# RMS norms that scale by a diagonal matrix inside the transposing products, with split passes held behind the norm's steps

## The chip, the cores and the metric

The kernel runs on one core of a Trainium2 chip. The metric is the device time of one execution in microseconds (us), smaller is better. The kernel before takes 2280.77 us, the median of 3 runs (2278.39 to 2280.96).

## The reference, cut to what matters

Two blocks of two layers each run on 256 tokens of width 1024, all in float32. Every large product is preceded by an RMS norm of the residual x; these norms are what the change rewrites.

```python
def rms_norm(x, w):
    y = x * lax.rsqrt(jnp.mean(x * x, axis=-1, keepdims=True) + EPS)
    return y * w
# first block, layers i = 0, 1
h = rms_norm(x, norm_mix_w[i])
mem_n = rms_norm(mem, mem_norm_w[i])
proj = h @ w_in[i]                       # gated delta rule (i=0), sparse attention (i=1)
x = x + concat([mix(proj), memory_attention(proj, mem_n)]) @ w_out[i]
x = x + conv_glu(rms_norm(x, norm_ffn_w[i]), w_up, conv_w, conv_b, w_down)
# second block, layers l = 0, 1; shift, scale and gate come from cond @ w_ada + b_ada
x = rms_norm(x, final_norm_w)            # between the blocks
h = rms_norm_2(x, norm1_g[l]) * (1 + scale1) + shift1
x = x + gate1 * (merged(h @ w_in[l]) @ w_out[l])
h2 = rms_norm_2(x, norm2_g[l]) * (1 + scale2) + shift2
x = x + gate2 * hierarchical_moe(h2)     # 32 experts
```

## The kernel before, in words

Everything is issued by one Python class in program order; a tile scheduler puts each engine's instructions in an order of its own, by dependences and its cost estimates, and each engine then runs its list strictly in that order. Weights come in units of 1 MB, tiles `raw` of 128 x 2048, loaded by SyncE (`unit`, L396) into a ring of four slots. Float32 products are made of three matmuls (`mm3`, L352 to L356): both operands are split into a high part and a low part, and high x high, high x low and low x high are summed. The split of a weight half (1024 columns) is a copy on ScalarE (L407) and a subtraction on VectorE (L408), into tiles `whl`, of which there are four (`split`, `hilo`). A unit is thus two splits and 48 matmuls of 256 columns (`ws2`).

The activations are split once per norm, into `xh` and `xl`, eight slices k of 128 features by 256 tokens. A norm goes like this. `sums_sq` (L523) squares x on ScalarE in four pieces (two token tiles tt, two halves) with an accumulated sum. `rms` adds EPS with a GpSimd tensor_scalar (L535) and takes the power -1/2 on GpSimd (`pow_half`, L510). `to_c_in` transposes x by sixteen TensorE transposes against the identity (L555), transposes the broadcast 1/rms into a row by two more (L560), copies that row to SBUF on ScalarE (`rsrow`, L561), multiplies each slice with weight and row on VectorE (`nf`, L567), and splits the slice: `xh` on ScalarE (L407), `xl` on VectorE (L408). In the second block, where there is a shift b, xh and xl are made with the bias (L571, L572). Then the next product's matmuls can start.

Six such norms stand between two stages of products, so that TensorE has nothing else: before the gated delta rule (`gdn`, the start of the program), before conv_glu of layer 0 and of layer 1, before the sparse attention, and before layers 0 and 1 of the second block (`layer2`). The first of those two is joined with the norm between the blocks (`mid_norm`, L594 to L596, and its `finish`, L602, which rescales x). This text calls them the six pauses. Two more norms (of mem) and the last one stand beside other work.

In both conv_glu's the modulation of the second block is computed on the side: `ada` loads 24 units `adaw` per layer on the same SyncE queue and adds each up on VectorE (L1172, the first of a group L1174), a few per chunk c of the eleven chunks (list NADA). At the program's start `start` and `masks` load x, the constants and four masks before the first weight unit is asked for (L638 to L641, L349, L396).

Of the kernel before, what the change touches and what calls it, by code (L numbers as in the profile page):

```python
# [38 lines left out]
GAP = 6  # L39
NADA = (2, 3, 2, 3, 2, 3, 2, 3, 3, 3, 3)  # L40
# [260 lines left out]
class Net:  # L301
    def __init__(self, ctx, tc, I, out, dbg=None):
# [11 lines left out]
        self.dtag = "acc"  # L314

# [83 lines left out]
    def split(self, src, n=1024):  # L399
        t = self.spl.tile([128, 2, 1024], F32R, name="whl")  # L400
        hi, lo = t[:, 0, :n], t[:, 1, :n]
        self.hilo(hi, lo, src)
        return hi, lo

    def hilo(self, hi, lo, src):

        self.nc.scalar.activation(hi, src, AF.Copy)  # L407
        self.nc.vector.tensor_sub(lo, src, hi.bitcast(F32))  # L408
# [103 lines left out]
    def sums_sq(self, x, tt, weight=None):  # L512
# [4 lines left out]
        for h in range(2):  # L517
            s = slice(h * 512, h * 512 + 512)
            if weight is None:
# [3 lines left out]
            nc.scalar.activation(junk, x[:, tt, s], AF.Square, scale=1.0 / math.sqrt(D), accum_out=ms[:, h:h + 1])  # L523
# [5 lines left out]
    def rms(self, x):  # L529

        rs = self.P.tile([128, 2], F32, name="rs", bufs=2)
        for tt in range(2):
            ms = self.sums_sq(x, tt)
# [5 lines left out]
    def to_c(self, x, rs, w, b, X, tag="mm"):  # L539

        self.nm += 1
        with self.tc.tile_pool(name=f"nrm{self.nm}", bufs=1, side="right", reuse_waits="tile") as tmp:
            return self.to_c_in(tmp, x, rs, w, b, X, tag)

    def to_c_in(self, tmp, x, rs, w, b, X, tag):
        nc, (xh, xl) = self.nc, X
        row = tmp.tile([128, 256], F32, name="rsrow")
        ps = []

        def rows():  # L550
            for _ in range(KB // 2):
                ps.append(self.pst([128, 2, 256], tag=tag))
            for tt in range(2):
                for k in range(KB):
                    nc.tensor.transpose(ps[k // 2][:, k % 2, tt * 128:tt * 128 + 128], x[:, tt, k * 128:k * 128 + 128], self.ident)  # L555

        def scales():
            p = self.dense([128, 256])
            for tt in range(2):
                nc.tensor.transpose(p[:, tt * 128:tt * 128 + 128], rs[:, tt:tt + 1].to_broadcast([128, 128]), self.ident)  # L560
            nc.scalar.activation(row, p, AF.Copy)  # L561

        for part in (scales, rows) if tag == self.dtag else (rows, scales):
            part()
        for k in range(KB):
            f = tmp.tile([128, 256], F32, name="nf", bufs=2)
            nc.vector.scalar_tensor_tensor(f, ps[k // 2][:, k % 2, :], w[:, k:k + 1], row, op0=OP.mult, op1=OP.mult)  # L567
            if b is None:
                self.hilo(xh[:, k, :], xl[:, k, :], f)
            else:  # L570
                nc.scalar.activation(xh[:, k, :], f, AF.Identity, bias=b[:, k:k + 1])  # L571
                nc.vector.scalar_tensor_tensor(xl[:, k, :], f, b[:, k:k + 1], xh[:, k, :].bitcast(F32), op0=OP.add,  # L572
                                               op1=OP.subtract)
# [5 lines left out]
    def norm_x(self, x, w, X=None):  # L579

        return self.to_c(x, self.rms(x), w, None, X or self.xtiles(), self.dtag if X else "mm")

    def mid_norm(self):
# [7 lines left out]
        for tt in range(2):  # L591
            ms = self.sums_sq(self.x, tt, w2)
            r, a = rs[:, tt:tt + 1], r1[:, tt:tt + 1]
            nc.gpsimd.tensor_scalar(a, ms[:, 0:1], ms[:, 1:2], EPS, op0=OP.add, op1=OP.add)  # L594
            nc.gpsimd.tensor_scalar(r, a, EPS, ms[:, 2:3], op0=OP.mult, op1=OP.add)
            nc.gpsimd.tensor_scalar(r, r, ms[:, 3:4], None, op0=OP.add)  # L596
# [35 lines left out]
    def start(self):  # L632
# [7 lines left out]
        nc.sync.dma_start(self.consts, self.I["consts"][:, :NKEEP])  # L640
        nc.sync.dma_start(self.cols, self.I["cols"])  # L641
# [1204 lines left out]
```

## Time and profile before

| | us |
|---|---|
| median of 3 runs | 2280.77 |
| the profiled execution's own time | 2276.92 |
| its span in the trace | 2275.1 |
| busy: TensorE (PE) / VectorE (DVE) / ScalarE (ACT) / GpSimd (POOL) | 1941.0 / 1069.9 / 773.1 / 113.8 |
| mean granted TensorE clock | 0.916 of full |
| read from HBM | 649.93 MB |

The profiled execution lies 3.9 us below the median of the three runs, and about 1.8 us of its time lie outside the span. How to read the rows further down: times are counted from the start of the span; PE is TensorE's matmuls, PEld its weight loads, SPq the queue that issues DMAs. A timeline row gives the start, the length, the engine, line and operation, output <- inputs, the number of such instructions in a row, and in brackets the idle time before it and what ended that. Matmul ends are modelled, so the spacing of starts tells more than the lengths.

### The profile page before, as it was taken

How to read it: one execution, taken by the hardware profiler on the slowest of the kernel's cores; microseconds unless marked ns; L12 is line 12 of the kernel's file. 1: busy time of each engine (PE TensorE's matmuls, PEld its weight loads, DVE VectorE, ACT ScalarE, POOL GpSimd, SP SyncE). 2: the span in 40 equal slices, each digit the busy share in tenths (PEclk: the TensorE clock that was granted, in tenths of full speed). 3: DMA queues.
4: the chain of work that ended last, by engine and by line, in shares of the span. 5: the costliest groups of instructions: out<-in, count | busy, mean ns of one | idle time of the engine just before them, and what ended most of it. 6: DMA issues, size and time to landing. Idle time of an engine off the chain costs nothing. (4 is left out here: it accounts for less than half of the span.)

```text
span 2275.1 us, 31431 instructions
## 1 busy us (share of the span) xinstructions
PE 1941.0 (85%) x12792; PEld 1352.2 (59%) x12793; DVE 1069.9 (47%) x1912; ACT 773.1 (34%) x1343; POOL 113.8 (5%) x159
## 2 busy tenths in 40 slices
PE   7999999998998999899987666757899996777765
PEld 6999879987986998777942111112778831112121
DVE  6554479875547887776541111101876531111011
ACT  7577545443554544555410000000645410000000
POOL 1001000001000000101100000000020000000000
PEclk8999999999999999999999888887999998786777
DMA  6322268964426886435799999999555699999997
GB/s 228 129 94 80 89 243 318 334 247 159 181 75 240 304 317 243 158 144 224 272 384 420 420 421 421 420 420 389 200 204 231 255 406 421 421 421 420 420 386 325
DMA packets 96834, 653.17 MB, mean 287 GB/s; under 512 B 11640, under 2 KB 15392, under 8 KB 19112
## 3 DMA queue, kind: packets, MB, share of 16 engines
q1 hardware_dynamic: 96680, 651.05, 72.8%
q8 instruction: 105, 1.72, 0.3%
q14 instruction: 49, 0.40, 0.0%
HBM read 649.93 MB, written 1.08 MB: 286 GB/s over the span
## 5 line engine op out<-in xcount | busy, mean ns | idle before, releaser
L408 DVE TENSOR_TENSOR whl<-raw,whl 128x1024 fp32r<-128x1024 f32 x342 | 423.3, 1245 | 144.9 <-ACT whl L407 144.0
L407 ACT ACTIVATE whl<-raw 128x1024 fp32r<-128x1024 f32 x342 | 359.9, 1056 | 294.9 <-PE acc L356 149.5
L1644 PE MATMUL mm<-raw,q_XT 128*32 128x512 f32 x1808 | 278.7, 724 | 118.2 <-DMA raw<-in_moe 118.0
L354 PE MATMUL acc<-xh,whl 128*128 128x256 f32 x784 | 226.3, 293 | 9.7 <-ACT xh L407 6.5
L1644 PEld LDWEIGHTS mm<-raw,q_XT 128*32 128x32 f32 x1808 | 46.9, 117 | 308.4 <-DMA raw<-in_moe 183.8
L1637 ACT ACTIVATE q_XT<-mm,mc,modA 128x128 f32<-128x128 f32 x64 | 29.3, 458 | 587.7 <-DVE q_XT L1639 369.6
L356 PE MATMUL acc<-xh,whl 128*128 128x256 f32 x784 | 225.1, 290 | 1.4 <-DVE whl L408 1.4
L355 PE MATMUL acc<-xl,whl 128*128 128x256 f32 x784 | 225.7, 290 | 0.6 <-DVE xl L572 0.6
L355 PE MATMUL mm<-xl,whl 128*128 128x256 f32 x704 | 202.4, 288 | 4.6 <-DVE xl L408 4.6
L354 PE MATMUL mm<-xh,whl 128*128 128x256 f32 x704 | 201.6, 288 | 0.2
L356 PE MATMUL mm<-xh,whl 128*128 128x256 f32 x704 | 201.1, 286 | 0.0
L354 PEld LDWEIGHTS acc<-xh,whl 128*128 128x128 f32 x784 | 151.9, 196 | 14.9 <-ACT xh L407 7.1
L355 PEld LDWEIGHTS acc<-xl,whl 128*128 128x128 f32 x784 | 152.3, 195 | 2.1 <-issue 0.9
L356 PEld LDWEIGHTS acc<-xh,whl 128*128 128x128 f32 x784 | 151.5, 194 | 3.1 <-DVE whl L408 2.2
L355 PEld LDWEIGHTS mm<-xl,whl 128*128 128x128 f32 x704 | 137.0, 195 | 7.2 <-DVE xl L408 6.4
L354 PEld LDWEIGHTS mm<-xh,whl 128*128 128x128 f32 x704 | 137.0, 195 | 4.4 <-issue 1.7
L356 PEld LDWEIGHTS mm<-xh,whl 128*128 128x128 f32 x704 | 137.2, 195 | 0.1
L1644 PE MATMUL mm<-raw,q_aT 128*32 128x512 f32 x592 | 84.9, 660 | 29.0 <-DMA raw<-in_moe 25.4
L1678 DVE TENSOR_TENSOR q_y<-mm,gate 128x512 f32<-128x512 f32 x32 | 22.1, 692 | 184.3 <-PE mm L1644 184.3
L1667 DVE TENSOR_TENSOR q_a<-q_a,mm 128x512 f32<-128x512 f32 x16 | 11.0, 688 | 202.1 <-PE mm L1644 202.1
L1172 DVE SCALAR_TENSOR_TENSOR adas<-adaw,cond,adas 128x2048 f32<-128x2048 f32 x42 | 98.6, 2347 | 13.0 <-DMA adaw<-in_ada 13.0
L1664 DVE COPY q_WT<-mm 128x256 f32<-128x256 f32 x16 | 6.8, 424 | 198.4 <-PE mm L1662 198.4
(546 smaller groups left out, 3460.9 us busy)
## 6 DMA issues: line engine op xcount, KB each, us to landing
raw<-in_moe SPq DMA_DIRECT2D x300, 1024.0 KB, 19.9
raw<-in_ffn SPq DMA_DIRECT2D x66, 1024.0 KB, 5.0
whl<-in_moe SPq DMA_DIRECT2D x56, 1024.0 KB, 19.8
adaw<-in_ada SPq DMA_DIRECT2D x48, 1024.0 KB, 9.0
raw<-in_gmga SPq DMA_DIRECT2D x16, 1024.0 KB, 4.9
rawxh<-in_moe SPq DMA_DIRECT2D x14, 1024.0 KB, 19.8
rawxl<-in_moe SPq DMA_DIRECT2D x14, 1024.0 KB, 19.8
raw<-in_gqkv SPq DMA_DIRECT2D x12, 1024.0 KB, 4.9
```

Of the source, the lines that this page charges most:

```text
L354: mm(out, lh, rh, start=start, stop=False)
L355: mm(out, lh, rl, start=False, stop=False)
L356: mm(out, ll, rh, start=False, stop=stop)
L407: self.nc.scalar.activation(hi, src, AF.Copy)
L408: self.nc.vector.tensor_sub(lo, src, hi.bitcast(F32))
L1172: nc.vector.scalar_tensor_tensor(a, t, c, a, op0=OP.mult, op1=OP.add)
L1637: nc.scalar.activation(XT[:, k, :], p, AF.Identity, bias=B[:, k:k + 1], scale=A[:, k:k + 1])
L1644: mm(out[s, :], lhs[:, s], ut[:, 512 * e:512 * e + 512], start=start, stop=stop, tile_position=(0, 32 * e))
L1664: nc.vector.tensor_copy(WT, pt)
L1667: nc.vector.tensor_mul(a, a, gu[1])
L1678: nc.vector.tensor_mul(y, p, gate[:, h * 512:h * 512 + 512])
```

## The change

It has five parts.

1. **The diagonal.** VectorE multiplies the identity by 1/rms of a token tile (`diag`), and x is multiplied with that by ordinary float32 matmuls, which transpose and scale at once. The row transposes, `rsrow` and, where there is no shift, `nf` go. `xh` and `xl` are made straight from PSUM (ScalarE with the weight as scale, VectorE with scalar_tensor_tensor). With a shift, `nf` is made on VectorE and ScalarE in turn. The norms of conv_glu use the accumulators "acc" in place of "mm".
2. **GpSimd's additions.** The tensor_scalars of `rms` and `mid_norm` go to VectorE; the power stays on GpSimd.
3. **Lists of splits.** After each norm the next four weight splits may be issued only behind named steps of the norm (`holds`: behind the last square and diagonal, behind slice 3, or behind the last xh and xl). issue_after orders instructions on the same engine and adds no wait.
4. **Other work behind the norm.** In chunk 0 of conv_glu the `ada` steps, and between the blocks the rescaling of x, are issued behind the last xl.
5. **The start.** The first weight unit is asked for right behind the constants; the masks come in one DMA, later; 14 dummy matmuls run first; token tile 1 is squared on VectorE.

The diff, cut to its core:

```diff
+NWARM = 14
     def split(self, src, n=1024):
...
-        self.hilo(hi, lo, src)
+        with ExitStack() as st:
+            for i in self.holds.pop(0) if self.holds else ():
+                st.enter_context(self.tc.issue_after(i.ins))
+            self.hilo(hi, lo, src)
     def sums_sq(self, x, tt, weight=None, vec=False):
...
+            if vec:
+                nc.vector.tensor_tensor_reduce(out=junk, in0=x[:, tt, s], in1=x[:, tt, s], scale=1.0 / D, scalar=0.0,
+                                               op0=OP.mult, op1=OP.add, accum_out=ms[:, h:h + 1])
+            else:
+                self.last_sq = nc.scalar.activation(junk, x[:, tt, s], AF.Square, scale=1.0 / math.sqrt(D),
+                                                    accum_out=ms[:, h:h + 1])
     def rms(self, x, vec=None):
...
-            self.nc.gpsimd.tensor_scalar(r, ms[:, 0:1], ms[:, 1:2], EPS, op0=OP.add, op1=OP.add)
+            self.nc.vector.tensor_scalar(r, ms[:, 0:1], ms[:, 1:2], EPS, op0=OP.add, op1=OP.add)
             self.pow_half(r)
     def to_c_in(self, tmp, x, rs, w, b, X, tag, hold):
...
-                    nc.tensor.transpose(ps[k // 2][:, k % 2, tt * 128:tt * 128 + 128], x[:, tt, k * 128:k * 128 + 128], self.ident)
...
+        for tt in range(2):
+            self.last_diag = nc.vector.tensor_scalar_mul(diag[:, tt], self.ident, rs[:, tt:tt + 1])
+            for k in range(KB):
+                nc.tensor.matmul(ps[k // 2][:, k % 2, tt * 128:tt * 128 + 128], x[:, tt, k * 128:k * 128 + 128],
+                                 diag[:, tt], start=True, stop=True)
         for k in range(KB):
-            f = tmp.tile([128, 256], F32, name="nf", bufs=2)
-            nc.vector.scalar_tensor_tensor(f, ps[k // 2][:, k % 2, :], w[:, k:k + 1], row, op0=OP.mult, op1=OP.mult)
+            p, wk = ps[k // 2][:, k % 2, :], w[:, k:k + 1]
             if b is None:
-                self.hilo(xh[:, k, :], xl[:, k, :], f)
+                self.last_xh = nc.scalar.activation(hi, p, AF.Copy, scale=wk)
+                self.last_xl = nc.vector.scalar_tensor_tensor(lo, p, wk, hi.bitcast(F32), op0=OP.mult, op1=OP.subtract)
             else:
+                f = tmp.tile([128, 256], F32, name="nf", bufs=2)
+                if k % 2:
+                    nc.scalar.activation(f, p, AF.Identity, bias=b[:, k:k + 1], scale=wk)
+                else:
+                    nc.vector.tensor_scalar(f, p, wk, b[:, k:k + 1], op0=OP.mult, op1=OP.add)
+                self.last_xh, self.last_xl = self.hilo(hi, lo, f)
+            if k == 3:
+                half = self.last_xh, self.last_xl
+        if hold is not None:
+            first, all = (self.last_sq, self.last_diag), (self.last_xh, self.last_xl)
+            self.holds = [(first if hold == 1 else ()), ((), half, first)[hold], all, all]
     def start(self):
...
         nc.sync.dma_start(self.consts, self.I["consts"][:, :NKEEP])
+        self.ahead0 = [self.unit(self.I["gqkv"][4])]
         nc.sync.dma_start(self.cols, self.I["cols"])
     def conv_glu(self, l):
...
-            X = self.norm_x(self.x, self.col(f"ffn{l}"))
+            X = self.norm_x(self.x, self.col(f"ffn{l}"), tag="acc")
...
-                for _ in range(NADA[c]):
-                    next(ada, None)
+                with self.tc.issue_after(self.last_xl.ins) if c == 0 else ExitStack():
+                    for _ in range(NADA[c]):
+                        next(ada, None)
     def gdn(self):
+        self.warm(NWARM)
+        X = self.norm_x(self.x, self.col("mix0"), vec=1, hold=1)
     def layer2(self, l):
-            X = self.to_c(self.x, rs, A1, B1, self.xtiles())
-            finish()
+            X = self.to_c(self.x, rs, A1, B1, self.xtiles(), hold=2)
+            with tc.issue_after(self.last_xl.ins):
+                finish()
```

VectorE at the norm of conv_glu(1), before; `xres` are the additions that finish x, `whl` weight splits, `adas` steps of the modulation:

```order
657 L719 TENSOR_TENSOR xres<-xres,acc 128x512 x4
658 L408 TENSOR_TENSOR whl<-raw,whl 128x1024 x2
659 L567 SCALAR_TENSOR_TENSOR nf<-mm,cols,rsrow 128x256 x2
660 L408 TENSOR_TENSOR xl<-nf,xh 128x256
661 L567 SCALAR_TENSOR_TENSOR nf<-mm,cols,rsrow 128x256
662 L408 TENSOR_TENSOR xl<-nf,xh 128x256
663 L1174 TENSOR_SCALAR adas<-adaw,cond_7153 128x2048
664 L408 TENSOR_TENSOR xl<-nf,xh 128x256
665 L567 SCALAR_TENSOR_TENSOR nf<-mm,cols,rsrow 128x256 x2
666 L408 TENSOR_TENSOR xl<-nf,xh 128x256
667 L1172 SCALAR_TENSOR_TENSOR adas<-adaw,cond_7153,adas 128x2048
```

The same place in the change:

```order
653 L746 TENSOR_TENSOR xres<-xres,acc 128x512 x3
654 L547 TENSOR_SCALAR rs<-ms 128x1
655 L562 TENSOR_SCALAR diag<-consts,rs 128x128
656 L746 TENSOR_TENSOR xres<-xres,acc 128x512
657 L547 TENSOR_SCALAR rs<-ms 128x1
658 L562 TENSOR_SCALAR diag<-consts,rs 128x128
659 L571 SCALAR_TENSOR_TENSOR xl<-acc,cols,xh 128x256 x8
660 L1210 TENSOR_SCALAR adas<-adaw,cond 128x2048
661 L413 TENSOR_TENSOR whl<-raw,whl 128x1024 x2
662 L1208 SCALAR_TENSOR_TENSOR adas<-adaw,cond,adas 128x2048
```

The eight xl's now stand in one run, with neither nf nor adas nor whl among them; the adas steps come behind.

SyncE's queue in conv_glu(1), before, where `adaw` are the modulation's units and `raw` the weights:

```order
86 L396 DMA raw<-in_ffn 128x2048 x5
87 L1167 DMA adaw<-in_ada 128x2048 x5
88 L396 DMA raw<-in_ffn 128x2048
89 L1167 DMA adaw<-in_ada 128x2048 x2
90 L396 DMA raw<-in_ffn 128x2048 x2
91 L1167 DMA adaw<-in_ada 128x2048 x2
92 L396 DMA raw<-in_ffn 128x2048 x2
93 L1167 DMA adaw<-in_ada 128x2048
```

The same place in the change:

```order
82 L398 DMA raw<-in_ffn 128x2048 x5
83 L1203 DMA adaw<-in_ada 128x2048 x5
84 L398 DMA raw<-in_ffn 128x2048 x3
85 L1203 DMA adaw<-in_ada 128x2048 x2
86 L398 DMA raw<-in_ffn 128x2048 x2
87 L1203 DMA adaw<-in_ada 128x2048
88 L398 DMA raw<-in_ffn 128x2048
89 L1203 DMA adaw<-in_ada 128x2048 x2
```

Behind the first five adaw's, three raw units now stand ahead of the next adaw, where it was one.

SyncE's queue at the start, before:

```order
2 L638 DMA xres<-in_x 128x1024
3 L639 DMA xres<-in_x 128x1024
4 L640 DMA consts<-in_consts 128x417
5 L641 DMA cols<-in_cols 128x587
6 L349 DMA k_mincl<-in_consts 128x128
7 L488 DMA smallw<-in_gba 128x128
8 L338 DMA row_dt<-in_rows 128x8
9 L338 DMA row_alo<-in_rows 128x8
10 L349 DMA k_dm<-in_consts 128x384
11 L349 DMA k_band_266<-in_consts 128x128
12 L396 DMA raw<-in_gqkv 128x2048 x2
```

The same place in the change:

```order
2 L649 DMA xres<-in_x 128x1024
3 L650 DMA xres<-in_x 128x1024
4 L651 DMA consts<-in_consts 128x417
5 L398 DMA raw<-in_gqkv 128x2048
6 L653 DMA cols<-in_cols 128x587
7 L493 DMA smallw<-in_gba 128x128
8 L340 DMA row_dt<-in_rows 128x8
9 L340 DMA row_alo<-in_rows 128x8
10 L398 DMA raw<-in_gqkv 128x2048 x2
```

The first weight unit moved from the ninth transfer to the fourth, and the other two stand ahead of k_dm and k_band.

## Rows read from the trace of the kernel before

**Rows 1.** Busy time by stretch: stretch, length, PE, PEld, DVE, ACT, POOL busy, clock, DMA share, GB/s.

```profile
322.00:528.00 206.00, 204.06 (x1441) 189.20 (x1440) 171.40 (x183) 104.47 (x134) 5.58 (x4) 1.00 0.78 285
...
1142.00:1595.00 453.00, 319.88 (x1978) 99.43 (x1977) 75.92 (x212) 26.14 (x55) 2.37 (x6) 0.85 1.00 412
```

**Rows 2.** The same view, four shorter stretches.

```profile
311.00:317.90 6.90, 5.81 (x24) 5.21 (x25) 6.62 (x11) 1.77 (x5) 0.00 (x0) 0.51 1.00 423
...
716.60:720.60 4.00, 1.49 (x14) 1.25 (x12) 2.91 (x3) 2.41 (x6) 1.27 (x2) 1.00 0.81 285
720.60:730.80 10.20, 9.20 (x37) 7.88 (x37) 9.12 (x15) 3.23 (x8) 0.00 (x0) 0.50 1.02 422
...
1050.00:1080.00 30.00, 28.92 (x209) 22.55 (x207) 17.04 (x40) 16.38 (x41) 0.00 (x0) 1.00 0.31 107
```

**Rows 3.** Waits of PE: line, what for, us in total, times, longest.

```profile
PE acc L560 <- POOL rs L510: 10.5, 4, 3.9
```

**Rows 4.** Timeline of the pause before conv_glu(1).

```profile
716.03 0.39 PE L356 MATMUL acc<-whl,catl 128*128 128x512 f32 x1
...
716.46 0.69 DVE L719 TENSOR_TENSOR xres<-xres,acc 128x512 f32<-128x512 f32 x1 [0.67 <-PE acc L356]
...
718.30 0.61 ACT L523 ACTIVATE sq<-xres 128x512 bf16<-128x512 f32 x1
...
719.11 0.71 POOL L535 TENSOR_SCALAR rs<-ms 128x1 f32<-128x1 f32 x1 [2.79 <-ACT sq L523]
...
720.52 0.42 PE L560 MATMUL mm<-consts,rs 128*128 128x128 f32 x1 [2.51 <-POOL rs L510]
...
722.42 0.55 PE L354 MATMUL mm<-xh,whl 128*128 128x256 f32 x1
...
736.12 0.28 PE L356 MATMUL mm<-xh,whl 128*128 128x256 f32 x1
...
736.24 0.28 PE L354 MATMUL mm<-xh,whl 128*128 128x256 f32 x1
```

**Rows 5.** Timeline: the addition that finishes x, and the first matmul, at four other pauses.

```profile
305.78 0.68 DVE L719 TENSOR_TENSOR xres<-xres,acc 128x512 f32<-128x512 f32 x1
...
312.21 0.55 PE L354 MATMUL mm<-xh,whl 128*128 128x256 f32 x1
...
535.06 0.68 DVE L763 TENSOR_TENSOR xres<-xres,acc 128x512 f32<-128x512 f32 x1
...
542.01 0.58 PE L354 MATMUL acc<-xh,whl 128*128 128x256 f32 x1 [1.44 <-ACT xh L407]
...
926.16 0.68 DVE L763 TENSOR_TENSOR xres<-xres,acc 128x512 f32<-128x512 f32 x1
...
934.33 1.01 PE L354 MATMUL acc<-xh,whl 128*128 128x256 f32 x3 [1.53 <-ACT xh L571]
...
1595.52 1.28 DVE L1767 TENSOR_TENSOR xres<-xres,acc 128x512 f32<-128x512 f32 x2
...
1603.66 1.01 PE L354 MATMUL acc<-xh,whl 128*128 128x256 f32 x3 [1.53 <-ACT xh L571]
```

**Rows 6.** Single lines: count, shortest/median/longest ns, first and last start.

```profile
L1332 ACT ACTIVATE ymh<-mm,cols x8: 473/475/479, 1021.5 to 1692.3; 128x256 fp32r<-128x256 f32 x8
...
L1333 DVE SCALAR_TENSOR_TENSOR yml<-mm,cols,ymh x8: 475/484/486, 1022.0 to 1692.8; 128x256 fp32r<-128x256 f32 x8
```

**Rows 7.** Timeline: float32 products of 128x128 at the second block's first MoE.

```profile
1164.09 2.05 PE L1635 MATMUL mm<-q_P,xres 128*128 128x128 f32 x16
```

**Rows 8.** Timeline of the start: first weight split, first matmul of a product, end of three units.

```profile
12.50 1.06 ACT L407 ACTIVATE whl<-raw 128x1024 fp32r<-128x1024 f32 x1 [1.71 <-DMA raw<-in_gqkv]
...
15.71 0.58 PE L354 MATMUL acc<-xh,whl 128*128 128x256 f32 x1 [5.07 <-ACT xh L407]
...
41.07 0.38 PE L560 MATMUL acc<-consts,rs 128*128 128x128 f32 x2
```

**Rows 9.** The page's costliest groups: busy, mean ns, idle before.

```profile
L1172 DVE SCALAR_TENSOR_TENSOR adas<-adaw,cond,adas 128x2048 f32<-128x2048 f32 x42 | 98.6, 2347 | 13.0 <-DMA adaw<-in_ada 13.0
```

More of the change, by code (lines that the diff above doesn't have):

```diff
@@ L537, in rms, with to_c, to_c_in @@
         return rs
-    def to_c(self, x, rs, w, b, X, tag="mm"):
+    def to_c(self, x, rs, w, b, X, tag="mm", hold=0):
         self.nm += 1
         with self.tc.tile_pool(name=f"nrm{self.nm}", bufs=1, side="right", reuse_waits="tile") as tmp:
-            return self.to_c_in(tmp, x, rs, w, b, X, tag)
-    def to_c_in(self, tmp, x, rs, w, b, X, tag):
+            return self.to_c_in(tmp, x, rs, w, b, X, tag, hold)
+    def to_c_in(self, tmp, x, rs, w, b, X, tag, hold):
         nc, (xh, xl) = self.nc, X
[L547 to L554, printed above, removed]
-                    nc.tensor.transpose(ps[k // 2][:, k % 2, tt * 128:tt * 128 + 128], x[:, tt, k * 128:k * 128 + 128], self.ident)
[L557 to L564, printed above, removed]
@@ L565, in to_c_in @@
+        diag = tmp.tile([128, 2, 128], F32, name="diag")
+        ps = [self.pst([128, 2, 256], tag=tag) for _ in range(KB // 2)]
+        for tt in range(2):
[3 more added lines that the diff above has]
+                                 diag[:, tt], start=True, stop=True)
         for k in range(KB):
-            f = tmp.tile([128, 256], F32, name="nf", bufs=2)
@@ L650, in masks, with warm @@
         self.maskb = {}
-        for name in ("mincl", "mstrict", "mfwd", "mbwd"):
-            m = self.maskb[name] = P.tile([128, CONST.off[name][1]], BF, name=name)
-            with self.tc.tile_pool(name="mk" + name, bufs=1, reuse_waits="tile") as mp:
-                nc.gpsimd.tensor_copy(m, self.late(name, mp))
+        names = ("mincl", "mstrict", "mfwd", "mbwd")
+        o, n = CONST.off[names[0]][0], sum(CONST.off[name][1] for name in names)
+        with self.tc.tile_pool(name="mk", bufs=1, side="right", reuse_waits="tile") as mp:
+            t = mp.tile([128, n], F32, name="k_masks")
+            nc.sync.dma_start(t, self.I["consts"][:, o:o + n])
+            for name in names:
+                c, w = CONST.off[name]
+                m = self.maskb[name] = P.tile([128, w], BF, name=name)
+                nc.gpsimd.tensor_copy(m, t[:, c - o:c - o + w])
+    def warm(self, n):
+        nc = self.nc
+        with self.tc.tile_pool(name="cold", bufs=1, side="right", reuse_waits="tile") as tmp:
+            z = tmp.tile([128, 512], BF, name="cold")
+            nc.vector.memset(z, 0.0)
+            p = self.pst()
+            for _ in range(n):
+                nc.tensor.matmul(p, z[:, :128], z, start=True, stop=True)
     def mem_kv(self, l, m, X):
@@ L773, in gdn @@
             t28 = lambda name: pool.tile([128, 2, 8], F32, name=name)
-            pba = self.small(I["gba"], 16, X)
+            with tc.issue_after(self.last_xh.ins), tc.issue_after(self.last_xl.ins):
+                pba = self.small(I["gba"], 16, X)
             dtb, alog = self.row("dtb"), self.row("alog")
+            ahead = self.ahead0 + [self.unit(I["gqkv"][4 * j]) for j in (0, 2)]
             sp = pool.tile([128, 2, 16], F32, name="sp")
@@ L780, in gdn @@
             self.softplus(sp, ab)
-            nc.scalar.activation(alog, alog, AF.Exp)
+            with tc.issue_after(self.last_xh.ins):
+                nc.scalar.activation(alog, alog, AF.Exp)
             g, gc, gl = t28("g"), t28("gc"), pool.tile([128, 8], F32, name="gl")
@@ L793, in gdn @@
             nc.vector.memset(epsc, EPS)
-            pairs = [self.gdn_pair(u, X, pool, sp, gc, gl, epsc) for u in range(4)]
+            pairs = [self.gdn_pair(u, X, pool, sp, gc, gl, epsc, None if u else ahead) for u in range(4)]
+            self.masks()
             for step in range(3 * GAP + 20):
@@ L943, in gdn_pair @@
         pz = self.xs2(I["gz"][u], X)
-        nc.scalar.activation(zs, pz, AF.Silu)
+        silu = nc.scalar.activation(zs, pz, AF.Silu)
+        if u == 0:
+            self.cond = self.P.tile([128, 8], F32, name="cond")
+            with self.tc.issue_after(silu.ins):
+                nc.scalar.activation(self.cond, self.col("cond"), AF.Silu)
         po = self.pst([128, 4, 128])
@@ L1816, in run @@
             self.start()
-            self.masks()
             self.mixer(0)
```

39 lines of the change are left out of this document (19 added, 20 removed).

## The prediction

> **What bounds the kernel now.** I read the busy times by stretch first. Two kinds of stretch have different limits. In the stages of products PE is the bound: 204.06 of 206.00 us in conv_glu(0), with DVE at 171.40 and a clock of 1.00 [rows 1]. In the MoEs it is the DMA: share 1.00 and 412 GB/s over 453 us, PE busy 320 of them [rows 1]. The loading for the MoEs begins as the stage before frees its ring: its DMA share is 0.31 at 1050 to 1080 [rows 2]. So what PE gains ahead of it also brings the MoE forward, and a gain in a pause reaches the end.
>
> Then the waits of PE, for what lies between: in the pauses PE waits for the norm, above all for GpSimd's power in front of the row transposes, 10.5 us in four waits [rows 3]. The timeline of one pause shows the chain [rows 4]. Before conv_glu(1) the last matmul of the stage before starts at 716.03 and x is finished at 717.15 (716.46 + 0.69). The last square starts only at 718.30, as weight splits stand ahead of it on ACT; POOL adds at 719.11 for 0.71, the row is transposed at 720.52, and the first matmul of the next product follows at 722.42. The 48th of its matmuls starts only at 736.24, where 48 at the 0.12 between 736.12 and 736.24 [rows 4] would be 5.7 us, since DVE makes four adas steps of 2.35 us [rows 9] and a shorter first one between the xl's.
>
> Last I read the clock: 1.00 until 720.6, then 0.50, the lower of 2.4 and 1.2 GHz, until 730.8; ahead of the fall PE was busy 1.49 of 4.00 us. Before conv_glu(0) the halved stretch is 6.9 us with 24 matmuls in 5.81 busy us [rows 2], 0.24 each.
>
> **The change, by the steps of one pause.** From x finished to the first matmul, now, by the rows of the pause before conv_glu(1):
> - hop and last square to its sum: 0.05 + 0.81 (718.30 to 719.11 [rows 4]); the splits no longer stand between.
> - the addition on DVE: 0.2. The trace shows none of this form there, so it lies between nothing and the 0.48 that DVE takes for 256 columns [rows 6]; POOL's took 0.71 [rows 4]. I take a value near the low end, since it is one column.
> - POOL's power and its hops: 0.70 (719.11 + 0.71 to 720.52 [rows 4]).
> - the diagonal, 128 columns on DVE: 0.25, half of the 0.484 for 256 [rows 6], and 0.05 to hop.
> - two float32 products of the first slice: 0.27. Sixteen of this shape start within 2.05 us, 0.13 each [rows 7].
> - xh from PSUM with a scale: 0.475, as L1332 [rows 6], and 0.1 to hop.
>
> The sum is 2.9 us from x to the first matmul. Then a new xl comes every 0.48 at most (L1333 [rows 6]), eight in 3.9; 24 matmuls of a half-unit wait for them, and 24 more follow at 0.12 each, 2.9. So the 48th starts about 7 us behind the first; with a clock halved for 6.9 us, some 30 matmuls at 0.22 to 0.24 and the rest at 0.12, about 9. The removed nf, row copy and row transposes cost nothing more; what they took of DVE (0.48 x 8 a norm) is larger than what the diagonals add.
>
> **Rule against row.** Sixteen float32 products of 128 columns take 2.05 us at full clock [rows 7], hence 0.27 for two. The Trainium skill, FP8 and Floating Point Precision (TensorE Precision Notes), says that true FP32 needs four passes through the array: by that, as an estimate, 4 x 128 columns at 2.4 GHz are 0.21 us a product, sixteen are 3.4 us, and the sum would fall by about 0.2 us a pause, since from the second slice on products run under the xl's. The trace does not agree (0.13), and I go by the trace.
>
> **The sum**, each against the same place before:
> - conv_glu(1): the first matmul at 717.15 + 2.9 = 720.05 in place of 722.42; the 48th at 727 to 729 in place of 736.24 [rows 4], a gain of 7.2 to 9.2. But five adas steps (1.3 + 4 x 2.35 = 10.7 us) now stand behind the xl's, among the next splits that must come in time. In conv_glu(0) DVE has 206 - 171 us free [rows 1], 3 us in each of eleven chunks, so 10.7 are caught up in four, while the four whl tiles cover. I take 7; down to 3 if part of it is waited for.
> - conv_glu(0): x at 306.46, first matmul 309.4 in place of 312.21 [rows 5]; two adas steps leave the xl's too. 4.5 (2.8 to 5.7).
> - sparse attention: x at 535.74, 538.6 in place of 542.01 [rows 5]. 3.5 (2.8 to 4.6).
> - layer2(0): x at 926.84; the weighted sum of 512 columns adds one pass on DVE (0.7, as the addition to x), two more additions 0.4, and the slice with shift 0.5: 931.4 in place of 934.33 [rows 5]. But each slice has more passes (nf, xh, xl over two engines), so 2.5 (1.5 to 3.5).
> - layer2(1): x at 1596.80, with two squares behind it (1.6), so 1601.2 in place of 1603.66 [rows 5]. 2 (1.5 to 3).
> - the start: the first unit was split at 12.50, its product started at 15.71, and three units (168 matmuls with the small one, 20.2 us at 0.12) were done at 41.07 [rows 8], 25.4 after. Asked for ahead of six transfers, the unit is no longer last; the norm is, with the squares shared between ACT and DVE. I estimate a start at 10 to 10.5, and 23 after it: 33.5. That is 7.5. At the low end (4) only the start moves, by 4; at the high end (10) the clock is also kept up and nothing waits for xl. The 14 dummies (512 columns, 0.24 each at twice 0.12, 3.4 us, twice that at half clock) run while x and the constants are on their way, and cost nothing unless they outlast these.
> - the end (POOL's addition leaves the chain) and the two norms of mem: 1 (0 to 3).
> - SP and POOL: no DMA is added and three mask loads go. The masks come after mem, behind the first units; they are read only once the first products are there, so I cost that at nothing, a few us within the start's bound if they are late.
>
> In all 28 us, with bounds of 16 and 39. Against the profiled execution, 2276.9, that is 2249; that execution lies 3.9 below the median of 2280.8, against which it is 2253. I put the forecast between, at **2251**.
>
> **Rivals.**
> 1. *The clock stays up.* PE is busy 1.49 of 4.00 us before the clock falls [rows 2]; with 2.9 us from x to the matmul and products in between, it may not fall. A halved stretch of 6.9 us loses half of it; by the two lengths above (7 and 9 us to the 48th matmul) 2 us in each of five pauses. 28 + 10 gives **2241**. For it: the idle time shrinks by over 2 us. Against it: the pause still leaves PE with little to do for 3 us. The Trainium skill, TensorE: Matmul & The Clock Gate (Part 4), says that transposes do not count as busy in the way that matmuls do, which speaks for this rival, as sixteen transposes become matmuls; no row here separates the two.
> 2. *The delayed vector work comes back.* Behind each norm DVE owes two splits (2.5) and in the conv_glu's 3.6 and 10.7 of adas: 5 x 2.5 + 14.3, some 27 us. If PE waits for half of it, 14 are left: **2265**; if for all, nothing is gained: **2279**. Against it: DVE is busy 171 of 206 [rows 1] and PE's waits within that stage are under 2 us in all, so there is room.
> 3. *Slower: SP's queue stalls DVE.* In the change three raw units stand ahead of the next adaw in conv_glu(1), where it was one. SP waits at each raw for a slot that DVE's split frees, so an adaw is issued late, DVE (in order) waits for it, and the splits behind it wait too. DVE has 3 us free per chunk; from a wait above that PE stands still. At 5 us a chunk the loss is 2 us in each of twenty, 40, less the 28: **2290**. For it: DVE waits 13.0 us for adaw already [rows 9]. Against it: that is 0.3 a step over 42, and by the order four or more splits (5 us of DVE, 11 us of PE) stand between an adaw's issue and its use.
> 4. *The change does less than it says:* issue_after only orders, and the splits may have been harmless; then the pauses give 1.5 each and the start 4: **2267**.
>
> **How the numbers follow.** The forecast 0.60, rival 1 0.17, the half of rival 2 with rival 4 0.15, the whole of rival 2 0.05, rival 3 0.03. Faster by over 0.2% (4.6 us, about what a measurement here can tell) are the first three, 0.92; same 0.05; slower 0.03. The range takes the bounds of the sum, 2276.9 - 39 = 2238 and 2280.8 - 16 = 2265, and most of rivals 1, 2 and 4: 2235 to 2268.
>
> **What would show it.** Right: no POOL addition, no row transposes and no nf ahead of xh in four pauses; first matmul 4 to 4.5 us after the last one of the stage before; eight xl's in a row in about 3.6 us; three units at the start done at 33 to 34; conv_glu stretches still 99% PE; MoE stretches as long as now. Wrong: PE waits for whl in the chunk behind a norm (rival 2), DVE's waits for adaw far over 13 us (rival 3), or a first matmul that comes no earlier. The clock's rows at the pauses decide rival 1.

## The result and the profile after

The changed kernel takes 2263.88 us (median of 4, 2260.96 to 2265.22), the kernel before 2280.66 in the same comparison: ratio 0.9932, 95% interval 0.9918 to 0.9946, faster by some 15 us (its bounds 12 to 19). That is inside the range and 13 us above the forecast of 2251. The profiled execution takes 2260.96 us, span 2258.9.

Stretches that answer to [rows 1, 2], in the same columns: conv_glu(0) behind the pause, the pause before conv_glu(1) in two parts, the first MoE.

```profile
317.50:528.00 210.50, 207.30 (x1456) 192.37 (x1455) 172.06 (x181) 103.67 (x132) 1.06 (x2) 0.99 0.78 290
714.80:718.80 4.00, 3.16 (x26) 2.98 (x27) 1.32 (x4) 1.09 (x3) 0.55 (x1) 1.00 0.84 295
718.80:726.20 7.40, 7.11 (x58) 6.71 (x57) 6.71 (x11) 5.78 (x11) 0.00 (x0) 1.00 1.03 415
1129.80:1583.40 453.60, 327.72 (x1969) 100.50 (x1968) 75.88 (x212) 26.05 (x55) 2.35 (x6) 0.82 1.00 411
```

The MoE is as long as before (453.6 for 453), so what is gained ahead of it passes through. In the pause the clock stays at 1.00. But conv_glu(0) shows 3.2 us without PE work, where it was 1.9, and a clock of 0.99.

The waits of PE that are new or answer to [rows 3]:

```profile
PE mm L564 <- DVE diag L562: 8.4, 5, 2.5
...
PE acc L356 <- ACT ffh L412: 4.9, 4, 2.3
...
PE mm L505 <- ACT smallr L502: 3.7, 1, 3.7
...
PE acc L564 <- DVE diag L562: 2.5, 3, 1.4
...
PE mm L358 <- DVE whl L413: 1.4, 2, 0.7
```

The timeline of the pause that [rows 4] shows of before:

```profile
714.17 0.39 PE L358 MATMUL acc<-whl,catl 128*128 128x512 f32 x1
...
714.94 0.68 DVE L746 TENSOR_TENSOR xres<-xres,acc 128x512 f32<-128x512 f32 x1
...
715.71 0.63 ACT L534 ACTIVATE sq<-xres 128x512 bf16<-128x512 f32 x1 [0.97 <-DVE xres L746]
...
716.47 0.21 DVE L547 TENSOR_SCALAR rs<-ms 128x1 f32<-128x1 f32 x1 [0.85 <-ACT sq L534]
716.76 0.55 POOL L515 TENSOR_TENSOR rs<-rs,mhalf 128x1 f32<-128x1 f32 x1 [2.06 <-DVE rs L547]
717.35 0.29 DVE L562 TENSOR_SCALAR diag<-consts,rs 128x128 f32<-128x128 f32 x1 [0.66 <-POOL rs L515]
...
717.69 2.05 PE L564 MATMUL acc<-diag,xres 128*128 128x128 f32 x16 [0.56 <-DVE diag L562]
719.50 0.36 PE L356 MATMUL mm<-xh,whl 128*128 128x256 f32 x1
```

The square follows x at once, and the addition costs 0.21. From x (715.62) to the first matmul it is 3.88 us, where it was 5.27 (717.15 to 722.42).

**Where the time came from.** In both kernels the three-part matmuls (`mm3`) number 6816. I set the start of the n-th one before against the n-th one of another execution; the difference, the lead, is what has been gained by then. These are my sums from the timelines. The second column of leads is the changed kernel's next profiled execution (first run below; span 2263.5).

| stretch (place in before) | forecast | gained, first | gained, second |
|---|---|---|---|
| start to 300 | 7.5 | -0.5 | -6.4 |
| pause, conv_glu(0), to 334 | 4.5 | 5.0 | 5.0 |
| the rest of conv_glu(0), to 529 | 0 | -4.4 | -2.5 |
| pause, sparse attention, to 548 | 3.5 | 3.5 | 3.5 |
| its stage, to 711 | 0 | -1.8 | -1.9 |
| pause, conv_glu(1), to 748 | 7 | 8.7 | 8.6 |
| the rest of conv_glu(1), to 920 | 0 | -1.6 | -1.6 |
| pause, layer2(0), to 959 | 2.5 | 3.4 | 3.6 |
| stage, MoE and pause of layer2(1), to 1618 | 2 | 0.8 | 1.2 |
| to the end of the span | 0.5 | 3.1 | 1.9 |

The first four pauses gave what was forecast or more. The fifth, of layer2(1), gave less: from x to its first matmul it is 5.61 us in the first execution and 6.67 in the second, where it was 6.86. The start gave nothing, and the stages behind the pauses took 6 to 8 us back. (The forecast's 1 us for the end and the norms of mem is halved here; the half for mem has no row.)

### The profile page after: what moved, and what is told of

It reads as the page before. It is cut to its first block, busy times and chain, and to the rows that moved or that the text cites. A ratio compares the mean times of both kernels' runs of the same rounds, so it can differ in the third digit from the quotient of the medians.

```text
span 2258.9 us, 31633 instructions
## 1 busy us (share of the span) xinstructions
PE 1943.6 (86%) x12918; PEld 1362.3 (60%) x12919; DVE 1058.1 (47%) x1899; ACT 770.9 (34%) x1336; POOL 99.7 (4%) x137
## 5 line engine op out<-in xcount | busy, mean ns | idle before, releaser
L1681 PE MATMUL mm<-raw,q_XT 128*32 128x512 f32 x1808 | 273.0, 712 | 115.0 <-DMA raw<-in_moe 114.8
L1674 ACT ACTIVATE q_XT<-mm,mc,modA 128x128 f32<-128x128 f32 x64 | 29.3, 458 | 589.8 <-DVE q_XT L1676 348.8
L1717 PE MATMUL acc<-q_y,q_WT 128*128 128x512 f32 x128 | 78.0, 741 | 22.8 <-DVE q_y L1715 22.0
```

What stands on the lines that cost most here:

```text
L1674: nc.scalar.activation(XT[:, k, :], p, AF.Identity, bias=B[:, k:k + 1], scale=A[:, k:k + 1])
L1681: mm(out[s, :], lhs[:, s], ut[:, 512 * e:512 * e + 512], start=start, stop=stop, tile_position=(0, 32 * e))
L1717: mm(accs[tt][h], WT[:, tt, :], y, start=first, stop=last)
```

## The experiments

All medians are of four or more runs beside the kernel before, which took 2278.84 to 2279.69 in these comparisons; the ratio is to that.

| run | median us | ratio, interval |
|---|---|---|
| the change again | 2263.77 | 0.9927 (0.9911 to 0.9942) |
| start as before | 2266.65 | 0.9936 (0.9915 to 0.9956) |
| no lists of splits | 2275.13 | 0.9983 (0.9972 to 0.9993) |
| transposes for the diagonal | 2266.62 | 0.9946 (0.9931 to 0.9961) |
| lists and put-off work alone | 2270.46 | 0.9966 (0.9954 to 0.9977) |
| adas not put off | 2257.18 | 0.9905 (0.9891 to 0.9920) |
| small product ahead of mem | 2259.56 | 0.9914 (0.9901 to 0.9926) |
| adas behind each ffl | 2288.81 | 1.0036 (1.0022 to 1.0050) |
| transposes and dummies | 2273.17 | 0.9977 (0.9968 to 0.9987) |
| adas not put off, small first | 2255.39 | 0.9897 (0.9881 to 0.9913) |
| the same, mem by transposes | 2252.20 | 0.9881 (0.9865 to 0.9896) |
| the run before this, all by transposes* | 2274.89 | 0.9980 (0.9971 to 0.9988) |

*with adas not put off and small first.

**1. The change again.**

> The changed kernel once more, unchanged, to see which of its features repeat. Both theories: 2261 to 2266 us, no lead over the kernel before left at 60 us. Theory A (the losses behind the pauses are single PE waits of 1 to 4 us, some of which lower the clock): the waits stand at the same places (20.4 to 24.4, 46.7 to 49.2, near 330 and near 472), while which of them lowers the clock may differ by execution. Theory B (the losses are the vector work that was put off): the same loss of 1 to 2 us in the first chunks behind each pause, with PE waiting for whl.

Measured 2263.77. The waits stand at the same places; the clock fell behind the wait at 857 in both executions and behind the one at 475 only in the first (lead lost there 2.2 and 0.2). The start differs by 6 us: here the clock is at 0.50 in three stretches between 25 and 70. So part of the table's differences is the clock of one execution, and the start's column must not be read from one.

**2. The start as before.** The four masks are again loaded and converted one by one ahead of the mixer; the core of the rest:

```diff
-        self.ahead0 = [self.unit(self.I["gqkv"][4])]
...
-        self.warm(NWARM)
-        X = self.norm_x(self.x, self.col("mix0"), vec=1, hold=1)
+        X = self.norm_x(self.x, self.col("mix0"))
...
-            with tc.issue_after(self.last_xh.ins), tc.issue_after(self.last_xl.ins):
-                pba = self.small(I["gba"], 16, X)
+            pba = self.small(I["gba"], 16, X)
```

> The start as before (order of the loads, masks, no dummies, squares of token tile 1 on ScalarE, no list of splits there), all the rest of the change kept. Theory A, by which the start's lead of 4 us is lost by 60 us and nothing is left: the time of the changed kernel, within 1.5 us, and at 60 us no lead either. If the start did give what the prediction put there, 4 to 7.5 us more than the changed kernel.

Measured 2266.65, 2.8 us more, between the two expectations. The runs lie from 2255.9 to 2270.4, so these times neither show a gain at the start nor exclude several us of one. The lead at 64 us is -2.4, in the change -0.5 and -6.3, and in no profile with the new start is it above 0.4 (run 10): the forecast's 7.5 never reached 64 us. The changed kernel's rows show what PE met instead:

```profile
9.52 1.06 ACT L412 ACTIVATE whl<-raw 128x1024 fp32r<-128x1024 f32 x1 [3.49 <-DMA raw<-in_gqkv]
...
11.67 2.67 ACT L570 ACTIVATE xh<-mm,cols 128x256 fp32r<-128x256 f32 x7 [1.09 <-DMA cols<-in_cols]
...
12.20 0.39 PE L356 MATMUL acc<-xh,whl 128*128 128x256 f32 x1
...
22.61 0.63 ACT L534 ACTIVATE sq<-mem 128x512 bf16<-128x512 f32 x1 [2.15 <-DMA mem<-in_mem]
...
23.99 0.36 ACT L502 ACTIVATE smallr<-mm 16x256 f32<-16x256 f32 x1
...
24.40 0.30 PE L505 MATMUL mm<-consts,smallr 16*128 16x16 f32 x2 [3.68 <-ACT smallr L502]
```

The first unit is split 3 us earlier than in [rows 8] and the first matmul comes 3.5 earlier. But cols, now behind the unit, holds xh for 1.09. Then ScalarE, in order, waits 2.15 for mem with the small product's copy queued behind it, and PE waits 3.68 for that copy. Run 7 takes both of these away and gains little, so they do not explain the lost lead by themselves.

**3. No lists of splits.**

```diff
-            self.holds = [(first if hold == 1 else ()), ((), half, first)[hold], all, all]
+            self.holds = []
```

> The change without the lists of splits (the scheduler places the splits as it likes). If the splits ahead of the squares and of the xl's cost what the rows of the kernel before suggest, 1 to 1.5 us more in each of five pauses, 2269 to 2271 us. If they were harmless (theory B: put off, they only come back), the changed kernel's time within 1.5 us.

Measured 2275.13, 11 us more than the change: above what was expected. ScalarE's rows in the pause before conv_glu(0):

```profile
307.69 0.61 ACT L534 ACTIVATE sq<-xres 128x512 bf16<-128x512 f32 x1
...
308.30 1.99 ACT L412 ACTIVATE whl<-raw 128x1024 fp32r<-128x1024 f32 x2
310.20 0.61 ACT L534 ACTIVATE sq<-xres 128x512 bf16<-128x512 f32 x1
```

Two splits (1.99) stand ahead of the last square, which starts 0.56 behind the end of x where it was 0.09 in the change. More is lost behind it (the clock falls at 314.5 too), by the splits on VectorE ahead of the addition and in GpSimd's power:

```profile
311.95 1.22 DVE L413 TENSOR_TENSOR whl<-raw,whl 128x1024 fp32r<-128x1024 f32 x1
312.12 1.46 POOL L515 TENSOR_TENSOR rs<-rs,mhalf 128x1 f32<-128x1 f32 x1 [6.40 <-DVE rs L547]
```

and in the change:

```profile
308.29 0.55 POOL L515 TENSOR_TENSOR rs<-rs,mhalf 128x1 f32<-128x1 f32 x1 [5.26 <-DVE rs L547]
```

The power took 1.46 us where a split was already running on VectorE, and ended 0.4 behind that split. It is the same in the pauses at 542.70 and 928.12 (1.45 and 1.46; 0.54 and 0.55 in the change). Over all fourteen traces, such a power took 1.38 to 1.47 us when a split, or the rescaling of x, was running as it started (14 cases), and 0.54 to 0.57 when the split began later (18 cases). So an order on VectorE also shortens a step of GpSimd; what lets the one hold up the other is not shown. By the leads the lists are worth 2.8 us in that pause, 0.7 and 0.8 in the next two and some 3.3 in layer2(0).

**4. Transposes for the diagonal**, with the row copy and nf as before; the work that waited for the last diag now waits for the last square.

```diff
-            self.last_diag = nc.vector.tensor_scalar_mul(diag[:, tt], self.ident, rs[:, tt:tt + 1])
-                nc.tensor.matmul(..., x[:, tt, k * 128:k * 128 + 128], diag[:, tt], ...)
+        self.last_diag = self.last_sq
+                nc.tensor.transpose(..., x[:, tt, k * 128:k * 128 + 128], self.ident)
+        nc.scalar.activation(row, p, AF.Copy)
+            nc.vector.scalar_tensor_tensor(f, ps[k // 2][:, k % 2, :], w[:, k:k + 1], row, ...)
```

> The change with transposes, row of scales and nf in place of the products with the diagonal; additions on VectorE, lists of splits, put-off work and start kept. By the steps of the prediction the chain to the first matmul is longer by some 1.2 us in each of six pauses, 7 us in all: 2271. If the products also are what keeps the clock up in the pauses (the prediction's rival 1), the clock falls to 0.5 behind at least three of the five later pauses again, 2 us more each: 2277 or more.

Measured 2266.62, below what was expected: 2.9 us more than the change, and the intervals overlap. The clock falls at 313.5, 542.2, 723.1 and 1586.7, as expected; three of these four do not show in the change's profiles. The pauses lose some 3 us each, as the 1.2 of the chain and the 2 of the clock together would have it (1.9 gained in place of 5.0 in conv_glu(0), 0.9 for 3.5, 5.1 for 8.7). But less is lost again behind them: 0.3 in conv_glu(0) in place of 4.4, and nothing in the sparse attention's stage and in conv_glu(1), in place of 1.8 and 1.6.

**5. Lists and put-off work alone**: the edits of runs 2 and 4, and the additions back on POOL. Only the lists, the put-off of adas and the accumulators of conv_glu's norms are left of the change.

```diff
-            self.nc.vector.tensor_scalar(r, ms[:, 0:1], ms[:, 1:2], EPS, ...)
+            self.nc.gpsimd.tensor_scalar(r, ms[:, 0:1], ms[:, 1:2], EPS, ...)
```

> The kernel before with the lists of splits and the put-off work (adas steps, rescaling) alone: transposes, row of scales, nf, additions on GpSimd and the start as before; only the accumulators of conv_glu's norms stay changed. Theory C (the order of the splits and of the put-off work is most of the gain, 10 to 12 us of it, and the diagonal about 3): 2267 to 2271 us. Theory D (the order pays only where the short chain of the diagonal makes room for it): 2275 us or more.

Measured 2270.46, ratio 0.9966, 8 us (5 to 10). The time is that of theory C, the share is less than it had: the order alone makes half of the gain, with no arithmetic changed. Run 3 keeps the short chain without the lists and gains 4 us, but it also keeps the put-off; what the chain gains with neither was not run.

**6. adas not put off.**

```diff
-                with self.tc.issue_after(self.last_xl.ins) if c == 0 else ExitStack():
-                    for _ in range(NADA[c]):
-                        next(ada, None)
+                for _ in range(NADA[c]):
+                    next(ada, None)
```

> The change without putting off the adas steps of the first chunk behind the last xl. If the steps between the xl's cost what the rows of the kernel before show (two waits of 1.6 us for xl in conv_glu(1), about one in conv_glu(0)) some 4 us more than the changed kernel: 2267 to 2269, with the lead behind the pause of conv_glu(1) 3 to 5 us smaller and nothing regained in the stage behind. If they only move, the same time within 1.5 us, as the stage behind returns it.

Measured 2257.18, 6.6 us *less* than the change; both expectations miss. The intervals overlap a little (0.9920 here is above the 0.9911 of run 1), so the size is uncertain by a few us, but runs 10 and 11, which keep this edit, lie as low. The leads of the pauses hardly differ (4.6 and 8.2), and the stages keep them: -0.4 in conv_glu(0), +2.6 in conv_glu(1). With the products and no nf the xl's come so close together that the scheduler itself puts the first adas step, 1.27 us, behind the seventh of the eight xl's and all the others behind the eighth. What the order edge changes is the rest of the stage. Near 470 in the change:

```profile
468.14 2.35 DVE L1208 SCALAR_TENSOR_TENSOR adas<-adaw,cond,adas 128x2048 f32<-128x2048 f32 x1 [1.74 <-DMA adaw<-in_ada]
...
473.46 0.68 DVE L772 TENSOR_TENSOR ffa<-ffa,mm 128x512 f32<-128x512 f32 x1
...
474.86 0.50 PE L356 MATMUL acc<-whl,ffh 128*128 128x512 f32 x1 [2.27 <-ACT ffh L412]
```

and without the edge:

```profile
468.65 2.34 DVE L1207 SCALAR_TENSOR_TENSOR adas<-adaw,cond,adas 128x2048 f32<-128x2048 f32 x1
...
472.44 0.68 DVE L772 TENSOR_TENSOR ffa<-ffa,mm 128x512 f32<-128x512 f32 x1
...
473.91 0.50 PE L356 MATMUL acc<-whl,ffh 128*128 128x512 f32 x1 [1.18 <-ACT ffh L412]
```

In the change an adas step waits for its unit with ffa queued behind it on VectorE, and PE waits 2.27 for ffh in place of 1.18. The waits near 330 and 738 for a split behind adas (0.7 each) are gone as well, and the clock stays at 1.00 behind both conv_glu waits.

**7. Small product ahead of mem**, with cols ahead of the first unit.

```diff
-        self.ahead0 = [self.unit(self.I["gqkv"][4])]
         nc.sync.dma_start(self.cols, self.I["cols"])
+        self.ahead0 = [self.unit(self.I["gqkv"][4])]
...
-        self.nc.scalar.activation(r[:n], p[:n, :256], AF.Copy)
+        self.last_small = self.nc.scalar.activation(r[:n], p[:n, :256], AF.Copy)
...
-        self.norm_x(m, self.col(f"mem{l}"), X)
+        with self.tc.issue_after(self.last_small.ins):
+            self.norm_x(m, self.col(f"mem{l}"), X)
```

> The change with the squares of mem ordered behind the copy of the small product on ScalarE, and cols asked for ahead of the first weight unit. Theory A1 (the start's lead is lost as ScalarE waits for mem's transfer ahead of that copy, and PE with it): the PE wait of 3 to 4 us at 20.4 to 24.3 falls under 1.5 us, the clock stays up at 25, the lead at 65 us is 2 to 4 us larger than in the changed kernel, time 2260 to 2262. Theory A2 (the chain of the delta rule behind it sets the time at 60 us in any case): the wait goes but the lead at 65 us does not change by more than 1 us.

Measured 2259.56; the interval overlaps that of the change again, so a gain is not shown. Rows of its start:

```profile
10.59 1.06 ACT L412 ACTIVATE whl<-raw 128x1024 fp32r<-128x1024 f32 x1 [4.57 <-DMA raw<-in_gqkv]
...
12.10 0.36 PE L356 MATMUL acc<-xh,whl 128*128 128x256 f32 x1
...
26.51 0.59 PE L820 MATMUL mm<-g,consts 128*128 128x8 f32 x4 [2.29 <-DVE g L817]
```

With cols first the unit's split comes 1 us later and stands ahead of xh on ScalarE, so the first matmul comes only 0.1 earlier. PE no longer waits for the copy (smallr at 20.68), but 2.29 us for the gates of the delta rule; the clock falls at 26.9 all the same and the lead at 64 us is -4.2, within the change's own -0.5 and -6.3. Theory A2 fits better: a wait was replaced by the next one in that chain. That the chain of the delta rule sets the time there was not tested.

**8. adas behind each ffl**, in every chunk.

```diff
-                self.hilo(ah, al, a)
+                ffl = self.hilo(ah, al, a)[1]
...
-                with self.tc.issue_after(self.last_xl.ins) if c == 0 else ExitStack():
+                with self.tc.issue_after(self.last_xl.ins if c == 0 else ffl.ins):
```

> The change with each chunk's adas steps ordered behind the chunk's ffl on VectorE. Theory A (the stage's losses are PE waits behind an adas step of 2.35 us that stands ahead of the product with val, and the clock that falls with them): the waits of 2.2 to 2.9 us before the wo matmuls near 472 and 856 go, the clock stays up there, 4 to 7 us less than the changed kernel: 2257 to 2260. Theory B (vector work put off comes back): PE waits for whl or ffh elsewhere in the chunks, the same time within 2 us.

Measured 2288.81, slower than before. PE waits elsewhere, in front of the products that sum up a group of steps:

```profile
PE mm L1185 <- DVE adas L1208: 19.3, 3, 6.7
```

PE's order was made with those products early, and PE, in order too, stands before them (5.86 us until 389.49) with the other matmuls queued behind. Theory B, by a way that I had not named.

**9. Transposes and dummies**: run 4, and behind the sixteen transposes of each norm with lists eight products that nobody reads.

```diff
+            d = self.dense([128, 512])
+            for _ in range(8):
+                nc.tensor.matmul(d, z[:, :128], z, start=True, stop=True)
```

> The kernel of the run with transposes (2266.6 us), with eight dummy matmuls of 512 columns behind the sixteen transposes of each of the six norms, in the time in which PE waits for the power. They add PE work and nothing else. Theory E (in the pauses the clock falls because PE does little, whatever the kind of its work): the clock stays at 1.00 at 313, 542, 723 and 1590 where it fell in that run, and the time is 4 to 8 us less, 2259 to 2263. Theory F (the products with the diagonal kept the clock up by being ordinary matmuls in the place of transposes, and the dummies come too late or too briefly for that): the clock falls as in that run, 2266 us or more.

Measured 2273.17. Stretches of the pause before conv_glu(0):

```profile
309.00:311.00 2.00, 2.00 (x12) 0.91 (x9) 0.33 (x2) 0.00 (x0) 0.55 (x1) 1.00 0.93 393
311.00:316.00 5.00, 2.65 (x13) 1.79 (x13) 4.12 (x10) 2.44 (x6) 0.00 (x0) 1.00 1.01 424
316.00:322.80 6.80, 6.72 (x30) 6.08 (x29) 6.51 (x11) 4.09 (x6) 0.00 (x0) 0.50 0.97 376
```

The dummies keep PE busy to 311 and the clock then holds 1.00 until 316, falling behind 5 us with PE busy 2.65: the time in which nf and xl come at 0.9 us a slice. So here the fall stands behind the slow slices, with the wait ahead of them filled. In the change PE is busy 7.11 of 7.40 in that part of its pause. The dummies do not only add PE work: in two pauses the row transposes stand behind them, 0.7 and 0.9 us after the power is done (310.68 after 309.96, 540.84 after 539.91), where it is under 0.1 in run 4. That is part of the 6.5 us by which this kernel is slower than run 4. The test does not separate the kinds of work: neither E nor F as put.

**10. adas not put off and small first**: the edits of runs 6 and 7.

> The adas steps of the first chunk not put off, and the squares of mem behind the small product's copy, with cols first: the two edits that each were faster than the change (2257.2 and 2259.6 against 2263.8). If both effects are real and separate, 2253 to 2256. If the second was within the scatter of the start, 2257 as with the first alone.

Measured 2255.39; not separable from 2257.18, so run 7's edit stays unproven.

**11. The same, with the norms of mem by transposes.** They alone have no list:

```diff
+        if hold is None:
...
+                        nc.tensor.transpose(..., x[:, tt, k * 128:k * 128 + 128], self.ident)
...
+            return X
```

> The run before this one, with the two norms of mem by transposes as in the kernel before. If a float32 product costs PE two instructions of 0.112 us and a transpose one of 0.109, this gives back 32 x 0.112 - 18 x 0.109 = 1.6 us of PE in conv_glu(0), of which the lead tables show 1.1, and up to as much at the start: 1 to 3 us less than that run. If the longer chain (row copy, nf) stands in the way of the first product with mem, the same or more.

Measured 2252.20, 3.2 us less, the expected direction and size, though the intervals overlap. Over mem's norm in conv_glu(0) its lead does 1.2 us better than run 10's. In the sparse attention's stage it does 3.3 better, as the clock did not fall near 560 in this execution; that this is the edit's doing is not shown. It is the fastest kernel here, faster than both: ratio 0.9881. The row behind it is the norm of mem in the change:

```profile
358.89 3.74 PE L564 MATMUL mm<-diag,mem 128*128 128x128 f32 x32
```

Sixteen products are 32 instructions, 0.112 apart.

**12. The same, all norms by transposes**: run 10 with the edit of run 4.

> The fastest kernel so far (2252.2 us: adas steps not put off, mem's squares behind the small product's copy, mem's norms by transposes), with transposes, row and nf in the six norms of x too. It prices the diagonal where nothing is put off behind it. Theory G (the diagonal shortens the pauses by some 8 to 10 us, as the leads behind the pauses say, and the change gave most of that back in the chunks behind by the put-off adas steps): 2260 us or more. Theory H (the diagonal itself is worth about 3 us, the difference between the change and the run with transposes): 2254 to 2257 us.

Measured 2274.89: 23 us more than run 11. Theory G's bound, by a larger amount, since another thing returns with the slower slices:

```profile
730.20 2.35 DVE L1217 SCALAR_TENSOR_TENSOR adas<-adaw,cond,adas 128x2048 f32<-128x2048 f32 x1
...
732.46 0.42 DVE L413 TENSOR_TENSOR xl<-nf,xh 128x256 fp32r<-128x256 f32 x1
...
732.93 0.58 PE L357 MATMUL mm<-xl,whl 128*128 128x256 f32 x1 [1.59 <-DVE xl L413]
```

With nf and xl in turn the scheduler again finds room for adas between them, so the diagonal's price here holds that too. The parts are not additive: with transposes the put-off is worth 8 us (2274.89 against 2266.62, which has the start of the change), with the diagonal it costs 6.6; the diagonal is worth 3 us with the put-off and some 20 without.

## Why the prediction was right, and where its terms were off

- **Bounds.** Right: MoE stretches as long as before, the pauses' gain passed through to the end.
- **The pauses.** Right in sum, partly by luck: 17.5 was forecast for the first four, some 20.6 came by the leads, while layer2(1) gave 0.2 to 1.2 of its 2. Two misses offset each other there: the chain is 1 us longer than the sum had it, and the clock, which the sum left halved behind each pause, stayed up. The readings of before also had a slip that did not matter: in conv_glu(1) three adas steps of 2.35 us stand between the xl's, not four (the fourth, at 735.76, follows the last xl), and 736.24 is the 47th matmul.
- **"Two float32 products of the first slice: 0.27", and the 2.9 us chain.** Wrong: 3.88. PE works in order, so the first matmul stands behind all sixteen instructions of the second token tile (1.8 us from 717.69 to 719.50), not two. It cost little, as the xl's set the pace: the 48th matmul came at 726.07, 10.4 from x, against 9.9 by the sum with the clock up.
- **Rule against row.** I misread [rows 7]: its sixteen are instructions, and a float32 product is two of them, as the 32 of run 11's row show: 0.224 a product. The Trainium skill, FP8 and Floating Point Precision (TensorE Precision Notes), with its four passes gives 0.21 (an estimate), and the trace agrees with that, not with my 0.13. In the pauses it mattered little. Mem's norm in conv_glu(0), where PE is the bound, lost 1.1 us by it, which my terms did not have.
- **"I estimate a start at 10 to 10.5, and 23 after it ... That is 7.5."** The step that failed most. The start came at 12.20, and its three units were done at 41.50, 29.3 after and no earlier than before, where the sum had 33.5. I priced SP's order and not who waits behind mem's transfer or cols. But run 7 removes both waits and its units are done at 40.97, so what holds PE behind them stays open; the gates of the delta rule, for which PE waits next, are the likely place. (Before, the unit is the eleventh transfer, not the ninth.)
- **"This is caught up in four chunks while whl's four tiles cover. I take 7"; rival 2.** The mechanism of rival 2 was real at a fourth of its price: 5 to 7 us in the two conv_glu's, shown by run 6. Spare VectorE time on average was no cover, because a single step of 2.35 us ahead of ffa makes PE wait, and the clock sometimes falls behind it (475.7 and 858.0 in one execution, only 861.9 in the other). Rival 3 appeared in small: two adas steps waited for their units (1.74 near 468, the other 4.0), in all 5.7 us in place of 13.0.
- **Rival 1** came true in part: in the change's two profiles no half-clock stretch in the first three pauses, but one each at 922.9 and 926.8 in layer2(0), and one at 1589.0 in layer2(1) of the second. What the clock gave is within the leads of the pauses above.
- **The number.** 2263.9 lies almost on rival 2's 2265, by other sums: some 8 us were missing at the start and 6 to 8 behind the pauses, most of it by the put-off work.
- **Signs.** Seen: no addition on GpSimd, no row transposes and no nf, MoE stretches as long as before. Not seen: the first matmul 4 to 4.5 us after the last one of the stage before (714.17 to 719.50, 5.3) and the start's units at 33 to 34. PE's waits for whl in a chunk behind a norm, a sign of being wrong, came to 1.4 us.
- **The lists** appear in my chain as "the splits no longer stand between". Taking them out costs 11 us (run 3), with the diagonal and the put-off in place. Lists and put-off alone give 8 (run 5); with transposes and the change's other parts, but adas not put off, they give 5 (run 12). The chain had no term for the power on GpSimd, which a running split lengthens by 0.9 us (run 3).

Not settled: the additions on VectorE, nf on two engines and the accumulators "acc", which have no run of their own; the 1.5 to 3.7 us that every kernel with the diagonal but run 11's (0.4) loses in the sparse attention's stage, where in most of them the clock falls near 560, and how much of the start's scatter is the clock alone.

## What to carry to other kernels

Keep work that nobody waits for out of the chain on every in-order queue; that alone was half the gain (run 5). Look beyond the queue too: a small GpSimd step took 0.9 us longer when it started under a long VectorE pass. But an order edge that is not needed for it can cost more than it gives (6.6 us here): look at who is queued behind the moved work a whole stage later, and measure each edge by itself and together with what it was made for. In the trace, count instructions per operation before taking a price from a row that says x16.

## What the runs showed of the hardware that I had not expected

A float32 128x128 product took two instructions of 0.112 us, a float32 transpose of the same shape one of 0.109. GpSimd's power over 128 x 1 took 0.54 to 0.57 us, but 1.38 to 1.47 when one of VectorE's 128-row passes over 1024 columns was already running as it started. And in the pause with dummies the clock fell from 1.00 to 0.50 behind a stretch in which PE was half busy with real work (2.65 of 5.00 us), although the wait ahead of it had been filled, so filling that wait did not save it.
